# Token sums of the four-group kernel as four spread actions, fewer weight-sum steps at the end of the first FFN

## The chip, the cores and the metric

The kernel runs on one core of a Trainium2 chip. The metric is device microseconds (us) of one execution, from its start to its end on that core; lower is better. TensorE (PE) does the matrix products, VectorE (DVE) and ScalarE (ACT) the elementwise work, GpSimd (POOL) some of it and part of the DMA issuing, and SyncE (SP) issues most loads. The trace gives TensorE's granted clock as a share of full speed.

## The reference

One layer of a decoder for 512 tokens with 1024 channels, in float32:

```python
h = x + 0.5 * swiglu(rmsnorm(h, norm_ffn1), ffn1_gate, ffn1_up, ffn1_down)   # hidden width 2816
u = rmsnorm(h, norm_mix)
parts = split(u @ w_in)             # queries, keys, values, branch gates, merge gates ga and gb
o_a = compressed + selected + windowed attention (8 heads)
o_b = sliding-window attention with sinks (8 heads)
h = h + (sigmoid(ga) * (o_a @ w_branch_a) + sigmoid(gb) * (o_b @ w_branch_b)) @ w_out
h = h + 0.5 * swiglu(rmsnorm(h, norm_ffn2), ffn2_gate, ffn2_up, ffn2_down)
out = rmsnorm(h, norm_final)
# swiglu(x, wg, wu, wd) = (silu(x @ wg) * (x @ wu)) @ wd
```

## The kernel before

**Products in parts.** TensorE rounds its operands, so each float32 operand is split in two: a high part (a cast, on ACT: `whi`, `uh`, `fhi`) and a low part (the operand minus its high part, a subtraction on DVE: `wlo`, `ul`, `flo`). Each product is three matmuls (high by high, low by high, high by low). A row tile is 128 channels by 512 tokens, and `KD` = 8 row tiles make the 1024 channels; a product of one row tile over all channels (`mm3`, L387) is so 24 matmuls. The residual `h` and the scaled activations `uh`, `ul` are held as eight such tiles, channels on partitions. Results stand in banks of PSUM named `acc`, `o`, `s` and (for transposes) `tp`, two of each.

**Weights.** Every product takes a block of 128 by 1024 weights from a ring in program order: SP loads it (`raw`, L143, 0.5 MB), ACT casts it (`whi`, L151), DVE subtracts (`wlo`, L155). There are four raw buffers, so a load is issued once the block four places earlier has been split.

**The stages, in order of time.** The first FFN (FFN1) in three thirds of hidden tiles, each with a down product of eight row tiles; the projection by `w_in` and the attention, whose order of tasks on PE is a list written out by hand; the merge of the two branches; the output projection by `w_out`, row tile by row tile (`d` from 0 to 7); the second FFN (FFN2) in three thirds of hidden tiles, `TILES = (4, 5, 0, 6, 7), (8, 12, 16), (17, 21)`; and the last down product with the final norm. Every engine has its own queue and does its instructions in the order in which the program issues them; nothing is reordered.

**Norms.** As each row tile of h is ready, `norm_in(d)` issues an ACT scale (`uh`, L653), a DVE subtraction (`ul`, L654), an ACT square (L664, in a buffer named `z`, `turn_a` and so on) and a POOL addition of the square to `sqacc` (L665). After the eighth, `norm_col` sums `sqacc` over the partitions with four small matmuls into `tp`, POOL takes the power (`ny`, L678), DVE finishes, and `norm_rows` makes the row factors `r_b` by which each product is multiplied afterwards (DVE, L1808 and L1815).

**Four-groups.** In FFN2 the tiles 0, 8, 12 and 17 stand for groups of four hidden tiles. The gate and up products of such a group are done as seven half-size products in place of eight (function `four`, products at L1875), from sums of weights and from sums of tokens. Their results are turned back to the layout of the rest by 12 groups of four transposes, `turn_back()` (L1911), which later products issue in between; a dictionary such as `up_at = {2: turn_back}` says after which of the eight steps of a product something is issued.

**Weight sums.** The sums of weights are made in DRAM by the DMA queue of POOL: 48 steps of 1 MB, each a copy (L401) or a copy that accumulates (L399), from the generator `sum_steps()`. Each `next(steps)` issues one step; a step that needs an earlier one waits for it on POOL's queue. The calls stand in FFN1 (after hidden tiles over 18, four, and in the last down product at d = 1, 3, 5), in attention (24, one every so many tasks), in the output projection (d = 1, 3, 5) and in FFN2 (after each tile and inside the four-groups), which has the other 14.

**Token sums.** For each of four pairs of row tiles (k and 4 + k), `sums_of_tokens` scales both (two on ACT), makes four half-width sums (DVE, L1729, L1730, L1734, L1735) and splits them (`fhi`, L390 on ACT, and `flo`, L391 on DVE). It does this in two calls per pair: scale, two sums, split; then two sums, split. The calls for k = 0 stand behind row tile 4 of the output projection (both), those for k = 1 behind row tiles 5 and 6; those for k = 2 and 3 behind the up product of the first and the second tile of FFN2, ahead of the reading of that product's bank (`t`, L1815).

**Elsewhere.** At the end of FFN1 each row tile of h is stored to DRAM (`hd`) for the output projection, since attention takes its space: the clearing of a buffer `turn_b` (POOL, L1020) is the first to use it. In FFN2, `residual(d)` transposes a row tile of h by PE (L2008) and copies it on ACT into `o_t`, the tile of the output.

Of the kernel before, what the change touches and what calls it, by code (L numbers as in the profile page):

```python
# [362 lines left out]
def layer(ctx, tc, a, out):  # L363
# [57 lines left out]
    def sum_steps():  # L421

        for pair in ((four_steps(FOURS[0]), down_sums(0)), (four_steps(FOURS[1]), four_steps(FOURS[2])),
                     (down_sums(8), four_steps(FOURS[3]))):
            for both_steps in zip(*pair):
                for y in both_steps:
                    issue(*y)
                    yield
# [379 lines left out]
    def ffn(after, begun, side, sums, early):  # L808
# [14 lines left out]
        for third, (f0, f1) in enumerate(THIRDS):  # L823
# [30 lines left out]
            for d in range(KD):  # L854
                po = acc(False)
                mm3(po, W.next(), g_in, f1 - f0)
                if third == 2 and d < KD - 1:
                    W.prep(W.pos + W.AHEAD)
                vector.scalar_tensor_tensor(h[:, d], po, 0.5, h[:, d], op0=OP.mult, op1=OP.add)
                if third == 0:  # L860
                    if d < 3:
                        sums_of_u(0, d + 1)
                    next(side, None)
                if third == 1 and d in (0, 2, 4, 6, 7):
                    next(early, None)
                if third == 2:
                    after(d)
                    if d in (1, 3, 5):
                        next(steps, None)
# [131 lines left out]
    with ExitStack() as mixing:  # L1001
# [717 lines left out]
        def sums_of_tokens(f, p0, names):  # L1719


            k, second = f // 2, f % 2
            tt, stt = vector.tensor_tensor, vector.scalar_tensor_tensor
            if not second:
                x, y = tokens["a"] = [p0.tile([128, S], F32, name=names[0]) for _ in range(2)]
                for o, d in ((x, k), (y, 4 + k)):
                    scalar.activation(o, h[:, d], AF.Identity, scale=gains[:, 2, d:d + 1])
                p = tokens["p"] = p0.tile([128, 2, 256], F32, name=names[1])
                tt(p[:, 0], y[:, 256:], x[:, 256:], op=OP.subtract)  # L1729
                tt(p[:, 1], x[:, :256], x[:, 256:], op=OP.subtract)  # L1730
            else:
                (x, y), s1 = tokens["a"], tokens["p"][:, 0]
                p = p0.tile([128, 2, 256], F32, name=names[1])
                stt(p[:, 0], s1, -1.0, x[:, :256], op0=OP.mult, op1=OP.subtract)  # L1734
                stt(p[:, 1], y[:, :256], -1.0, p[:, 0], op0=OP.mult, op1=OP.subtract)  # L1735
            split(four_hi[:, k, 2 * second:2 * second + 2], four_lo[:, k, 2 * second:2 * second + 2], p)

        with pool("merge", 2, side="right") as mp:
# [30 lines left out]
            m_in = (lambda k: mh[:, k]), (lambda k: ml[:, k])  # L1769
            for d in range(KD):  # L1770
# [4 lines left out]
                for i in {4: (0, 1), 5: (2,), 6: (3,)}.get(d, ()):  # L1775
                    sums_of_tokens(i, mp, ("z0", "z1"))
                if d in (1, 3, 5):
                    next(steps, None)


    with pool("temp3", 2) as temp, pool("end") as end:
# [62 lines left out]
        def four(j, pairs):  # L1844
# [3 lines left out]
            slot = {5: 0, 7: 1, 6: 2, 3: 3}  # L1848
# [239 lines left out]
        for third, tiles in enumerate(TILES):  # L2088
            if third == 2:
                make_room_again()  # L2090
            for n, f in enumerate(tiles):
# [6 lines left out]
                if n > 1 or third:  # L2098
                    gate_at = {2: turn_back, 6: turn_back}
                    up_at = {2: turn_back, 6: lambda: back(3 - third)}  # L2100
                z = []
                if third < 2:
# [9 lines left out]
                mm3(pu, W.next(), u_in, KD, rows if first else up_at)  # L2112
# [3 lines left out]
                if third == 0 and n < 2:  # L2116
                    for i in (4 + 2 * n, 5 + 2 * n):
                        sums_of_tokens(i, temp, ("y", "t"))
# [6 lines left out]
                gated(z[0], pu, f - THIRDS[min(third, 2) if f != 16 else 2][0], third == 0)  # L2125
                next(steps, None)
            if third < 2:
                down()
        for _ in last:
            pass  # L2130

# [24 lines left out]
```

## Time and profile before

| | |
|---|---|
| three runs | 1148.95, 1150.98, 1152.01 us (median 1150.98) |
| the profiled execution | 1150.53 us, its span 1148.8 us, mean granted clock 0.983 |
| PE busy | 1100.0 us (96%), 5827 matmuls |
| PE loading weights (beside products) | 940.4 us (82%) |
| DVE busy | 757.2 us (66%), 1358 instructions |
| ACT busy | 541.2 us (47%), 988 instructions |
| POOL busy | 219.7 us (19%), 253 instructions |
| HBM | 260 GB/s over the span |
| the hardware queue of SP's loads | 159.98 MB, 44.1% of the 16 DMA engines' time |
| the software queue of POOL | 67.11 MB, 25.0% of the 16 DMA engines' time |
| the chain that ended last | PE 81%, DVE 7%, DMA 6%, ACT 3%, issue 2% |

PE is busy nearly throughout. A busy PE is not PE at full speed, though: where the granted clock is 0.5, a matmul takes twice as long and still counts as busy. So the waits of PE, and the clock behind each of them, are to be read together. Times in what follows count from the start of the span.

### The profile page before, as it was taken

Reading aid. Unit: us, or ns where it says so; the run is one execution under the profiler, and the core shown is the slowest. Engines: PE = TensorE matmul, PEld = TensorE weight load, DVE = VectorE, ACT = ScalarE, POOL = GpSimd, SP = SyncE. Lnnn points to the kernel's source line nnn. Section 1 sums busy time; section 2 is a strip of 40 time slices with the busy share of each in tenths; the row PEclk is TensorE's granted clock in tenths of the full one; section 3 lists DMA queues with packets and bytes.
Section 4 is the critical chain, followed back from the end, with each engine's and each line's share of the span. In section 5 each row is a group of like instructions: output and inputs, shape, how many; then the busy total and the mean of one; then the engine's idle time right before and its main releaser. Section 6 shows DMA issues by size and latency. Waiting matters only on the chain.

```text
span 1148.8 us, 15814 instructions
## 1 busy us (share of the span) xinstructions
PE 1100.0 (96%) x5827; PEld 940.4 (82%) x5827; DVE 757.2 (66%) x1358; ACT 541.2 (47%) x988; POOL 219.7 (19%) x253
## 2 busy tenths in 40 slices
PE   9999998999999799999999999979779999999987
PEld 8888898988888798998888888867557888888876
DVE  5656785854656378896777466663547876887663
ACT  5434342542434256766667543454335445464432
POOL 0312111000003035654434432112000000000002
PEclk9999999999999899999999999998899999999999
DMA  6988989798659646737899556649993555646621
GB/s 208 264 223 207 257 185 323 216 324 272 197 198 235 159 107 187 148 147 205 286 228 311 154 177 208 154 147 234 289 285 127 190 193 163 194 142 196 205 73 74
DMA packets 201414, 232.44 MB, mean 202 GB/s; under 512 B 7924, under 2 KB 152120, under 8 KB 201016
## 3 DMA queue, kind: packets, MB, share of 16 engines
q1 hardware_dynamic: 172696, 159.98, 44.1%
q0 software_dynamic: 26176, 67.11, 25.0%
q10 hardware_dynamic: 2464, 4.33, 1.0%
q8 instruction: 46, 0.75, 0.3%
q14 instruction: 32, 0.26, 0.1%
HBM read 211.47 MB, written 87.03 MB: 260 GB/s over the span
## 4 chain that ended last, share of the span: by engine, by line
PE 81%; DVE 7%; DMA 6%; ACT 3%; issue 2%; POOL 0%; POOLq 0%; ACTq 0%; DVEq 0%; SPq 0%
PE acc L387 26%; PE o L387 18%; PE s L387 17%; PE o L1875 3%; PE acc L1875 3%; PE s L1875 3%; PE o L783 2%; PE tp L1643 2%; DMA raw<-in_ffn_gate_dram 2%; DVE wlo L155 2%; PE s L783 2%; PE acc L783 2%; DMA raw<-s 1%; ACT whi L151 1%; DMA raw<-in_ffn_up_dram 1%
## 5 line engine op out<-in xcount | busy, mean ns | idle before, releaser
L155 DVE TENSOR_TENSOR wlo<-raw,whi 128x1024 fp32r<-128x1024 f32 (+2 forms) x225 | 259.7, 1174 | 104.4 <-ACT whi L151 104.1
L151 ACT CAST whi<-raw 128x1024 fp32r<-128x1024 f32 (+2 forms) x250 | 228.9, 938 | 143.4 <-PE acc L387 22.7
L387 PE MATMUL acc<-uh,whi 128*128 128x512 f32 x224 | 91.3, 408 | 1.4 <-ACT whi L151 1.4
L387 PE MATMUL acc<-uh,wlo 128*128 128x512 f32 x224 | 88.7, 396 | 0.5 <-DVE wlo L155 0.5
L387 PE MATMUL acc<-ul,whi 128*128 128x512 f32 x224 | 88.3, 394 | 0.0
L387 PE MATMUL acc<-whi,uh 128*128 128x256 f32 x224 | 65.8, 294 | 1.2 <-ACT whi L151 1.2
L387 PE MATMUL acc<-wlo,uh 128*128 128x256 f32 x224 | 63.6, 284 | 0.1
L387 PE MATMUL acc<-whi,ul 128*128 128x256 f32 x224 | 63.6, 284 | 0.0
L2053 POOL TENSOR_TENSOR o_t<-o_t,g_b 128x512 f32<-128x512 f32 (+1 forms) x5 | 5.9, 1184 | 285.7 <-ACT z L2047 285.7
L1658 DVE TENSOR_TENSOR pts<-tp,pts 128x512 fp32r<-128x512 f32 (+1 forms) x62 | 41.9, 687 | 21.3 <-ACT pts L1655 20.6
L1557 ACT ACTIVATE pbuf<-s,m 128x256 f32<-128x256 f32 (+3 forms) x96 | 47.6, 503 | 8.4 <-DVE m L1549 4.0
L387 PEld LDWEIGHTS acc<-uh,wlo 128*128 128x128 f32 x224 | 42.5, 190 | 10.6 <-DVE wlo L155 1.4
L387 PE MATMUL acc<-G,whi 128*128 128x512 f32 x164 | 50.5, 389 | 0.0
L387 PEld LDWEIGHTS acc<-uh,whi 128*128 128x128 f32 x224 | 42.8, 191 | 9.2 <-ACT whi L151 1.8
L387 PE MATMUL s<-G,whi 128*128 128x512 f32 x160 | 49.4, 390 | 0.0
L387 PE MATMUL o<-uh,whi 128*128 128x512 f32 x120 | 48.8, 407 | 0.0
L387 PEld LDWEIGHTS acc<-ul,whi 128*128 128x128 f32 x224 | 42.7, 191 | 7.4
L387 PE MATMUL o<-G,whi 128*128 128x512 f32 x156 | 48.3, 390 | 0.4 <-DVE G L768 0.4
L387 PE MATMUL o<-ul,whi 128*128 128x512 f32 x120 | 47.5, 396 | 0.0
L387 PE MATMUL o<-uh,wlo 128*128 128x512 f32 x120 | 47.3, 394 | 0.0
L1655 ACT CAST pts<-tp 128x512 fp32r<-128x512 f32 (+1 forms) x62 | 35.5, 586 | 23.8 <-PE tp L1643 18.0
L1580 POOL TENSOR_SCALAR pbuf<-pbuf,c,gate 128x256 f32<-128x256 f32 (+3 forms) x57 | 34.8, 617 | 58.4 <-DVE c L1567 37.1
(471 smaller groups left out, 3039.7 us busy)
## 6 DMA issues: line engine op xcount, KB each, us to landing
raw<-in_ffn_gate_dram SPq DMA_DIRECT2D x42, 512.0 KB, 5.8
raw<-in_ffn_down_dram SPq DMA_DIRECT2D x34, 512.0 KB, 4.6
w<-in_ffn_up_dram POOLq DMA_DIRECT2D x16, 1024.0 KB, 11.3
raw<-w SPq DMA_DIRECT2D x32, 512.0 KB, 4.2
raw<-in_ffn_up_dram SPq DMA_DIRECT2D x30, 512.0 KB, 6.0
t<-in_ffn_down_dram POOLq DMA_DIRECT2D x12, 1024.0 KB, 12.6
raw<-in_w_in_dram SPq DMA_DIRECT2D x20, 512.0 KB, 9.1
raw<-s SPq DMA_DIRECT2D x16, 512.0 KB, 5.0
```

The source lines that it names most:

```text
L151: self.nc.scalar.copy(self.place(i)[0][:, k0:k1], self.raw[i][:, k0:k1])
L155: engine.tensor_tensor(lo, self.raw[i][:, k0:k1], f32(hi), op=OP.subtract)
L387: tensor.matmul(out, lhsT, rhs, start=start, stop=stop)
L783: tensor.matmul(o, a_[:, n], x(k), start=new and n == step == 0, stop=n == 7 and step == 2, skip_group_check=True)
L1557: scalar.activation(u.p[:, hd], b.view[:, j], AF.Exp, bias=u.m[:, hd:hd + 1], scale=-1.0, accum_out=u.sum[:, hd:hd + 1])
L1580: e.tensor_scalar(u.p[:, hd], u.p[:, hd], u.c[:, hd:hd + 1], u.gate[:, hd:hd + 1], op0=OP.mult, op1=OP.mult)
L1643: tensor.transpose(ps[:w, hd], u.p[:, hd, kb * w:kb * w + w], ident)
L1655: scalar.copy(p.hi, flat(b.ps)[:w])
L1658: vector.tensor_tensor(p.lo, flat(b.ps)[:w], f32(p.hi), op=OP.subtract)
L1875: tensor.matmul(ps, x, y[:, k], start=new and kk == k == step == 0, stop=kk == k == 1 and step == 2, skip_group_check=True)
L2053: gpsimd.tensor_tensor(y, y, left["g_b"][:, cs], op=OP.mult)
```

## The change

**Token sums.** `sums_of_tokens(k, p, name)` now returns four actions for a pair: `scaled` (two on ACT), `sums` (all four half-width sums on DVE, written over the two scaled tiles), `high` (two casts on ACT) and `low` (two subtractions on DVE). The kinds and the number of the instructions stay. The actions of a pair are issued a row tile apart in the output projection: for k = 0 behind row tiles 4, 5 and 6, for k = 1 behind row tiles 5, 6 and 7. In FFN2 they stand inside the gate and up products of the first two tiles, at given steps, and behind the reading of the up product's bank. Because the sums are made in place they stand in other slots of the operand, hence the new `slot`.

**Weight sums.** In the last down product of FFN1 only d = 1 issues a step, in the output projection d = 0 too. The 48 steps keep their order, so from there on every step is issued two places later; FFN2 has one more, 15.

**The last tile.** In the last third of FFN2, the gate product of tile 21 has no turn-backs inside it; two follow behind it, as before, and the other two stand inside the up product.

```diff
--- before.py
+++ after.py
@@ -425,7 +425,7 @@
             for both_steps in zip(*pair):
                 for y in both_steps:
                     issue(*y)
-                    yield
+                    yield True
 
     steps = sum_steps()
 
@@ -865,7 +865,7 @@
                     next(early, None)
                 if third == 2:
                     after(d)
-                    if d in (1, 3, 5):
+                    if d == 1:
                         next(steps, None)
         for g in (adds, side, early):
             for _ in g:
@@ -1716,24 +1716,34 @@
 
         tokens = {}
 
-        def sums_of_tokens(f, p0, names):
-
-
-            k, second = f // 2, f % 2
+        def sums_of_tokens(k, p, name):
+
+
+            pair = []
             tt, stt = vector.tensor_tensor, vector.scalar_tensor_tensor
-            if not second:
-                x, y = tokens["a"] = [p0.tile([128, S], F32, name=names[0]) for _ in range(2)]
-                for o, d in ((x, k), (y, 4 + k)):
+
+            def scaled():
+                pair.extend(p.tile([128, S], F32, name=name) for _ in range(2))
+                for o, d in zip(pair, (k, 4 + k)):
                     scalar.activation(o, h[:, d], AF.Identity, scale=gains[:, 2, d:d + 1])
-                p = tokens["p"] = p0.tile([128, 2, 256], F32, name=names[1])
-                tt(p[:, 0], y[:, 256:], x[:, 256:], op=OP.subtract)
-                tt(p[:, 1], x[:, :256], x[:, 256:], op=OP.subtract)
-            else:
-                (x, y), s1 = tokens["a"], tokens["p"][:, 0]
-                p = p0.tile([128, 2, 256], F32, name=names[1])
-                stt(p[:, 0], s1, -1.0, x[:, :256], op0=OP.mult, op1=OP.subtract)
-                stt(p[:, 1], y[:, :256], -1.0, p[:, 0], op0=OP.mult, op1=OP.subtract)
-            split(four_hi[:, k, 2 * second:2 * second + 2], four_lo[:, k, 2 * second:2 * second + 2], p)
+
+            def sums():
+                (x1, x2), (y1, y2) = ((t[:, :256], t[:, 256:]) for t in pair)
+                tt(y2, y2, x2, op=OP.subtract)
+                tt(x2, x1, x2, op=OP.subtract)
+                stt(x1, y2, -1.0, x1, op0=OP.mult, op1=OP.subtract)
+                stt(y1, y1, -1.0, x1, op0=OP.mult, op1=OP.subtract)
+
+            def high():
+                for i, t in enumerate(pair):
+                    scalar.copy(flat(four_hi[:, k, 2 * i:2 * i + 2]), t)
+
+            def low():
+                for i, t in enumerate(pair):
+                    hi, lo = (flat(o[:, k, 2 * i:2 * i + 2]) for o in (four_hi, four_lo))
+                    tt(lo, t, f32(hi), op=OP.subtract)
+
+            return scaled, sums, high, low
 
         with pool("merge", 2, side="right") as mp:
             mh, ml = (mp.tile([128, KD, S], F32R, name=n, bufs=1) for n in ("mh", "ml"))
@@ -1767,14 +1777,18 @@
                 split(mh[:, d], ml[:, d], y)
 
             m_in = (lambda k: mh[:, k]), (lambda k: ml[:, k])
+            first_sums = []
             for d in range(KD):
                 ps = acc(False)
                 mm3(ps, W.next(), m_in, KD)
                 vector.tensor_tensor(h[:, d], ps, h[:, d], op=OP.add)
                 norm_in(d, 2)
-                for i in {4: (0, 1), 5: (2,), 6: (3,)}.get(d, ()):
-                    sums_of_tokens(i, mp, ("z0", "z1"))
-                if d in (1, 3, 5):
+                if d == 4:
+                    first_sums.extend(sums_of_tokens(k, mp, "z%d" % k) for k in range(2))
+                    a0, a1 = first_sums
+                for action in {4: (a0[0],), 5: (a0[1], a1[0]), 6: (a0[2], a1[1], a0[3]), 7: (a1[2], a1[3])}[d] if d > 3 else ():
+                    action()
+                if d in (0, 1, 3, 5):
                     next(steps, None)
 
 
@@ -1845,7 +1859,7 @@
 
 
             home = {1: "acc", 2: "acc", 5: "s", 3: "s", 6: "o", 7: "o", 4: "o"}
-            slot = {5: 0, 7: 1, 6: 2, 3: 3}
+            slot = {5: 3, 7: 1, 6: 0, 3: 2}
             p, u, w, z, back_rows = [], [], [], [], []
             made = {1: (p, "z"), 5: (w, "t"), 6: (u, "s"), 2: (z, "y")}
             col, minus = norm["col"], norm["minus"]
@@ -2095,11 +2109,17 @@
                     continue
                 first = third == n == 0
                 gate_at, up_at = {}, {}
-                if n > 1 or third:
+                if third < 2 and n > 1:
                     gate_at = {2: turn_back, 6: turn_back}
+                if third or n > 1:
                     up_at = {2: turn_back, 6: lambda: back(3 - third)}
+                if third == 0 and n < 2:
+                    now = sums_of_tokens(2 + n, temp, "y")
+                    up_at = {1: now[0], 6: rows} if first else {1: now[1], 6: now[2]}
+                    if not first:
+                        gate_at = {1: before[2], 3: before[3], 5: now[0]}
                 z = []
-                if third < 2:
+                if third < 2 and not first:
                     up_at[4] = lambda: z.append(scaled(pg))
                 pg = acc(False)
                 wp = W.next()
@@ -2109,13 +2129,10 @@
                     back(2)
                     next(last)
                 pu = acc(False)
-                mm3(pu, W.next(), u_in, KD, rows if first else up_at)
+                mm3(pu, W.next(), u_in, KD, up_at)
                 if third == 0 and n < 2:
                     for d in range(4 * n, 4 * n + 4):
                         residual(d)
-                if third == 0 and n < 2:
-                    for i in (4 + 2 * n, 5 + 2 * n):
-                        sums_of_tokens(i, temp, ("y", "t"))
                 if third == 0 and n == 1:
                     make_room()
                 if third < 2 and n + 1 == len(tiles):
@@ -2123,11 +2140,15 @@
                 if not z:
                     z.append(scaled(pg))
                 gated(z[0], pu, f - THIRDS[min(third, 2) if f != 16 else 2][0], third == 0)
+                if third == 0 and n < 2:
+                    now[1 if first else 3]()
+                    before = now
                 next(steps, None)
             if third < 2:
                 down()
         for _ in last:
             pass
+        assert next(steps, None) is None
 
 
 _INS = ["x", "positions", "norm_ffn1", "ffn1_gate", "ffn1_up", "ffn1_down", "norm_mix", "w_in", "cmp_pe_k",
```

The next rows are POOL's, at the end of FFN1, the change against before: L399 are accumulating steps of the weight sums, `w_..` and `t_..` their sums in DRAM, and L665 adds a row tile's square to the norm's sum.

```order
 L399 DMA w_5_87<-in_ffn_up_dram 512x512
-L665 TENSOR_TENSOR sqacc<-sqacc,z 128x512 x2
-L399 DMA t_0_79<-in_ffn_down_dram 512x1x512
-L665 TENSOR_TENSOR sqacc<-sqacc,z 128x512 x2
-L399 DMA w_7_88<-in_ffn_up_dram 512x512
-L665 TENSOR_TENSOR sqacc<-sqacc,z 128x512 x2
+L665 TENSOR_TENSOR sqacc<-sqacc,z 128x512 x6
 L1020 MEMSET turn_b 64x512
```

Two steps have left the queue between the additions; they are now the first that attention issues.

The next rows are DVE's in the output projection, from the sums behind row tile 5 to the addition of row tile 7, first before: `z_..` are token sums, `wlo` a weight split, `h<-o,h` and `h<-s,h` the additions of row tiles 6 and 7.

```order
L1729 TENSOR_TENSOR z_7261<-z_7258,z_7257 128x256
L1730 TENSOR_TENSOR z_7261<-z_7257 128x256
L391 TENSOR_TENSOR flo<-z_7261,fhi 128x512
L155 TENSOR_TENSOR wlo<-raw,whi 128x1024
L1773 TENSOR_TENSOR h<-o,h 128x512
L654 SCALAR_TENSOR_TENSOR ul<-h,cols_c,uh 128x512
L1734 SCALAR_TENSOR_TENSOR z_7302<-z_7261,z_7257 128x256
L1735 SCALAR_TENSOR_TENSOR z_7302<-z_7258,z_7302 128x256
L391 TENSOR_TENSOR flo<-z_7302,fhi 128x512
L155 TENSOR_TENSOR wlo<-raw,whi 128x1024
L1773 TENSOR_TENSOR h<-s,h 128x512
```

After, from the addition of row tile 6 to that of row tile 7:

```order
L1784 TENSOR_TENSOR h<-o,h 128x512
L654 SCALAR_TENSOR_TENSOR ul<-h,cols_c,uh 128x512
L1732 TENSOR_TENSOR z_7251<-z_7251,z_7250 128x256
L1733 TENSOR_TENSOR z_7250<-z_7250 128x256
L1734 SCALAR_TENSOR_TENSOR z_7250<-z_7251,z_7250 128x256
L1735 SCALAR_TENSOR_TENSOR z_7251<-z_7251,z_7250 128x256
L1744 TENSOR_TENSOR flo<-z_7207,fhi 128x512
L1744 TENSOR_TENSOR flo<-z_7208,fhi 128x512
L155 TENSOR_TENSOR wlo<-raw,whi 128x1024
L1784 TENSOR_TENSOR h<-s,h 128x512
```

Between the two additions stand four sums of one pair and two low parts of the other, where before two sums, a low part and the casts between them stood; the casts that the low parts need are issued on ACT ahead of those sums.

The last rows are DVE's in the second tile of FFN2 (tile 5), up to the first four-group, first before: `z<-s` and `t<-acc` read the banks of the gate and the up product, `t<-y` and `t<-t,y` are token sums, `g` is the gated product.

```order
L1808 TENSOR_TENSOR z<-s,r_b 128x512
L1729 TENSOR_TENSOR t<-y 128x256
L1730 TENSOR_TENSOR t<-y 128x256
L391 TENSOR_TENSOR flo<-t,fhi 128x512
L1734 SCALAR_TENSOR_TENSOR t<-t,y 128x256
L1735 SCALAR_TENSOR_TENSOR t<-y,t 128x256
L391 TENSOR_TENSOR flo<-t,fhi 128x512
L1815 TENSOR_TENSOR t<-acc,r_b 128x512
L1824 TENSOR_TENSOR g<-s,t 128x512
```

After:

```order
L1822 TENSOR_TENSOR z<-s,r_b 128x512
L1829 TENSOR_TENSOR t<-acc,r_b 128x512
L1838 TENSOR_TENSOR g<-s,t 128x512
L1848 TENSOR_TENSOR g<-g 128x256
L1850 TENSOR_TENSOR g<-g 128x256
L1851 TENSOR_TENSOR left<-g,G 128x1024
L1852 TENSOR_TENSOR g<-g 128x256
L1853 SCALAR_TENSOR_TENSOR g<-g 128x256
L1855 TENSOR_TENSOR left<-g,G 128x768
L1744 TENSOR_TENSOR flo<-y,fhi 128x512 x2
L155 TENSOR_TENSOR wlo<-raw,whi 128x1024 x4
```

The reading of the up product's bank (`t<-acc`) now follows that of the gate's directly, and the fourth pair's low parts stand behind the gating, ahead of the weight splits of the four-group.

## The prediction

> **What bounds the kernel now.** I read the page first, then who waited for whom on TensorE (PE), then the stretches around its waits, then the chain that ended last inside them.
>
> ```profile
> span 1148.8 us, 15814 instructions
> PE tp L387 <- DVE sqacc L690: 6.0, 1, 6.0
> PE tp L387 <- POOL sqacc L665: 5.8, 1, 5.8
> PE acc L1875 <- DVE t L1815: 5.5, 1, 5.5
> PE tp L1911 <- DVE t L1861: 3.7, 4, 2.8
> ```
>
> The last four lines are the longest waits of PE (us in total, times, longest). Each of the first three is a single wait, and the change edits code ahead of each. The next view gives stretches: length, then busy time of PE, PEld, DVE, ACT and POOL, then the granted clock, DMA share and GB/s.
>
> ```profile
> 355.00:382.50 27.50, 27.07 (x156) 23.78 (x155) 12.93 (x14) 9.26 (x14) 9.74 (x8) 1.00 1.11 263
> 390.60:396.60 6.00, 5.97 (x28) 5.97 (x29) 3.25 (x10) 2.91 (x6) 0.00 (x0) 0.52 0.27 81
> 774.20:784.60 10.40, 10.39 (x34) 8.61 (x35) 4.09 (x12) 0.43 (x1) 5.36 (x6) 0.62 0.70 238
> 809.10:812.80 3.70, 3.70 (x9) 2.93 (x10) 2.93 (x5) 1.04 (x1) 0.00 (x0) 0.50 1.37 495
> 1094.30:1097.10 2.80, 0.00 (x0) 0.00 (x0) 2.61 (x5) 1.33 (x2) 0.00 (x0) 1.00 0.98 313
> ```
>
> After each of the three long waits PE runs at about half clock for some us: the loss is 6.0 x 0.48 = 2.9 us, 10.4 x 0.38 = 4.0 us and 3.7 x 0.50 = 1.9 us. The 2.8 us wait near the end leaves the clock at 1.00. By the Trainium skill ("TensorE: Matmul & The Clock Gate", What's actually happening) the clock halves after an idle window of about 3.4 us and comes back after about as much work; the five rows agree.
>
> **First term: the end of the first FFN.** This is the chain into the 6.0 us wait.
>
> ```profile
> 374.24 8.32 DMA hd<-h
> ...
> 382.74 0.53 POOL turn_b L1020
> ...
> 384.76 1.05 ACT whi L151
> ...
> 388.42 1.06 POOL ny L678
> ...
> 390.29 0.30 DVE sqacc L690
> ...
> 390.63 2.07 PE tp L387 x8
> ```
>
> The last store of h took 8.32 us. Everything behind it waits: POOL clears turn_b in the space that h leaves, ACT casts zeros from it and then two weight blocks, DVE splits these, and only then comes the norm that PE needs. Why was the store slow? The stretch 355 to 382.5 has DMA at 1.11, which is full. Two of the three weight-sum steps in flight there are those that the change takes out:
>
> ```profile
> 360.20 1.22 POOL L399 DMA_DIRECT2D t<-in_ffn_down_dram  x1
> 368.76 1.03 POOL L399 DMA_DIRECT2D w<-in_ffn_up_dram  x1
> ```
>
> ```profile
> q0 software_dynamic: 1584, 3.15, 33.8%
> ```
>
> ```profile
> DMA to landing us min/median/max: 3.2/7.0/11.4
> ```
>
> The second row is the queue of the weight sums between 340 and 392 us: three steps took 33.8% of 52 us, so 5.9 us of all engines each. Without two of them 11.7 us of transfers leave the queue ahead of the store. The third row is the eight stores of h: none landed in under 3.2 us. So the store gains at most 8.32 - 3.2 = 5.1 us; I take 4.6, since the loads of w_in and the stores remain. What is late next is the same chain, 1.4 us behind PE, too short a wait to lose the clock. Gain 4.6 + 2.9 = 7.5 us; ends: 1.0 (the store waits for other traffic) and 8.0.
>
> The two steps are not gone. Every step in attention now stands two places later, so two accumulations (5.9 us of DMA each) run where copies ran, and the last of the attention's steps move to the output projection (one more there) and one into the second FFN. In attention I cost this at nothing: its PE is covered by queued work. Its price there is from -2 to +3 us.
>
> **Second term: the output projection and the first tiles of the second FFN.** The chain as it stands:
>
> ```profile
> 737.10 5.44 PE o L387 x24
> ...
> 757.80 0.72 ACT uh L653
> ...
> 760.30 0.46 DVE z L1729
> ...
> 762.74 1.23 DVE wlo L155
> 763.96 0.61 DVE h L1773
> ...
> 766.11 1.46 DVE z L1734
> ...
> 770.79 0.70 DVE h L1773
> ...
> 772.14 0.62 ACT turn_a L664
> ...
> 772.89 1.28 POOL sqacc L665
> ...
> 774.21 1.87 PE tp L387 x8
> ```
>
> ```profile
> 753.42 0.42 DVE L1734 SCALAR_TENSOR_TENSOR z<-z,z 128x256 f32<-128x256 f32 x1
> ...
> 754.99 0.69 DVE L391 TENSOR_TENSOR flo<-z,fhi 128x512 fp32r<-128x512 f32 x1 [0.69 <-ACT fhi L390]
> ```
>
> A row tile's product is 24 matmuls in 5.44 us, 0.227 us each. PE stood still from 774.2 - 5.8 = 768.4, after 18 matmuls of the next product, so the last row tile's product ended at about 764.2 and its h could have been added then; DVE did it at 770.8, since it stood behind a ping-pong of ACT and DVE that one token sum needs within one row tile (scale, subtract, cast, subtract, then the same for the second half). The number of instructions on ACT and DVE does not change; their places do. I walk DVE's new order with these durations (0.42 for a half-width sum, 0.69 for a low part, 0.72 and 0.62 for ACT's scale and square): h of tile 6 at 759.1, its ul until 761.3, four sums with about 1 us lost beside POOL's add (the 1.46 row is such a case) until 763.8, two low parts until 765.1, a weight split until 766.4, h of tile 7 until 767.0, then ACT until 768.4 and POOL until 769.7. PE waits 1.3 us and not 5.8, and the clock holds: 4.5 + 4.0 = 8.5 us.
>
> Next comes the 5.5 us wait, on DVE's reading of a product's bank, which stood behind a token sum:
>
> ```profile
> 808.44 0.61 DVE t L1815
> ...
> 816.42 9.21 DMA raw<-in_ffn_up_dram
> ```
>
> ```profile
> PE s L1875 <- DVE wlo L155: 1.0, 2, 0.5
> ```
>
> In the new order that reading comes directly behind the product, so 5.5 + 1.9 us go. But two casts of the fourth token sum now stand on ACT ahead of the copies of the transposed residual, which gives PE about 2.0 us of waiting among its transposes. And two low parts (1.4 us) stand on DVE ahead of the weight split that the group's second product needs, which with ACT's later start makes PE wait about 4.4 us there, where it waits 1.0 now (the second fence, from the waits between 800 and 830). Net 5.5 + 1.9 - 2.0 - 3.4 = 2.0. PE so reaches the second product of the first four-group 10.5 us earlier. If those 4.4 us count as one gap, the Trainium skill's rule just named halves the clock once more; an estimate from the 1.9 us row then gives 1133.5.
>
> From there on loads set the pace:
>
> ```profile
> 825.73 1.05 ACT L151 CAST whi<-raw 128x1024 fp32r<-128x1024 f32 x1 [6.79 <-DMA raw<-in_ffn_up_dram]
> 852.14 1.05 ACT L151 CAST whi<-raw 128x1024 fp32r<-128x1024 f32 x1 [2.96 <-DMA raw<-w]
> ```
>
> ```profile
> q0 software_dynamic: 4896, 14.68, 78.1%
> ```
>
> ```profile
> q0 software_dynamic: 378, 1.42, 16.0%
> ```
>
> The first two rows are the first and the last of eight weight blocks cast in that stretch: (852.14 - 825.73) / 7 = 3.8 us apart, where PE uses one in 2.72. The third row says why: between 777 and 857 us the queue of weight sums alone takes 78% of all DMA engines. POOL has nothing else to do after the norm and issues all 14 steps left as fast as they chain. The change makes that 15; the fourth row (750 to 775 us) prices a copy at 25 x 0.16 / 1.42 = 2.8 us for a MB. The flood starts with the norm, so some 4 us earlier, and ends about when it does now. What matters for PE is the spacing of its own loads, and the four-group lies inside the flood before and after. I keep 10.5 us less half of the added copy, 1.4, for its meeting the loads: 9.0 us in round figures, ends 2 and 12.
>
> **Third term: the last tile.** Four turn-backs are groups of four transposes that wait for the four-group's last gating on DVE. Two of them stood inside the gate product.
>
> ```profile
> 1097.12 0.33 PE L1911 MATMUL tp<-ident,t 128*128 128x128 f32 x1 [2.83 <-DVE t L1861]
> ```
>
> This wait began at 1094.3, six matmuls and two transposes into the gate product, which so began at about 1092.5. Now all its 24 matmuls (5.4 us) run ahead of the first transpose, until about 1098, and the gating is done by then. The other two groups move into the up product, which ends at 1098 + 5.4 + 2 for the transposes = 1105.4; their low parts stand behind three weight splits of 1.2 us on DVE and land at about 1105.8, and the last products need the first of them 9 matmuls in, at 1107.4. Gain 3.0 us (the 2.8 and a little of the other three waits), ends 1 and 3.7.
>
> **Sum.** 7.5 + 9.0 + 3.0 = 19.5 us. The profiled execution took 1150.5 us (its span and 1.7 around it), 0.5 under the median shown: 1150.5 - 19.5 + 0.5 = 1131.5 us.
>
> **Rivals.** *The flood takes the second gain back.* DMA is full from 780 to 857, so an earlier PE only waits longer for the same bytes. For it: shares above 1. Against: the loads keep 3.8 us spacing while the sums hold 78%. Gain there 2 us: 1150.5 - 7.5 - 2 - 3 + 0.5 = 1138.5. The Trainium skill ("DMA: Bandwidth & Descriptors", Queues, rings and completion order) has each engine go round the queues packet by packet; by that rule the loads keep their share however long the flood is, which speaks against this rival.
>
> *The store of h stays late*, behind w_in's loads. Gain there 1 us: 1138. For it: the stores stand among w_in's loads, and one of them took 11.4 us. Against: DMA at 1.11 with 5.9 us of it per step.
>
> *The new order keeps DVE busy past tile 7* (the four sums are a dependent chain, in place), so the 5.8 us and its clock stay: second term 0.5, 1140. For it: DVE's walk has 1.3 us of lateness already. Against: the longest ping-pong is gone from its queue.
>
> *Slower.* The flood now begins with three copies in flight and may starve PE's loads. The first four-group would have to end 23 us later than my walk has it to bring the whole to 1154.5; with eight loads that decides from (26.4 + 23) / 7 = 7.1 us between loads, near double the spacing now; at 7.5 the time is 1157. Nothing shows such a spacing.
>
> **How the numbers follow.** Forecast 0.60 (alone 1126 to 1137); flood 0.14; store 0.10; DVE 0.06; two of these together, 1143 to 1147, 0.05; better than 1122, 0.02; slower 0.03. The range 1122 to 1142 takes in the first four. 0.3% is about 3.5 us, what a measurement of this kernel tells from no change. Under 1147.5: 0.94; within: 0.03; over 1154.5: 0.03.
>
> **What would show it.** In the changed profile: the store of h landing in 3 to 5 us, and PE's wait on sqacc L690 at 1 to 2 us with no stretch near half clock behind it; PE's wait on POOL's last sqacc under 2 us; no wait of over 3 us on the reading of a bank in tile 5; new waits on the residual's copies and ahead of the group's second product; the cast of that group's eight blocks still near 3.8 us apart, ending some 9 us earlier against the last row tile; no wait of PE in the last gate product. The prediction is wrong if the store still takes 8 us, if the group's spacing grows past 5 us, or if attention loses more than 3 us to the two moved accumulations.

## The result, and the profile after

| | before | changed |
|---|---|---|
| median of six runs | 1151.49 us | 1142.13 us |
| ratio of the runs compared | 1 | 0.9918, 95% interval 0.9893 to 0.9943 |
| the profiled execution, its span | 1150.53, 1148.8 us | 1139.69, 1138.0 us |
| mean granted clock | 0.983 | 0.987 |

One run of the changed kernel took 3404.14 us; the ratio leaves it out, while the median of six takes it in (1141.34 us without it). By the ratio the change is worth 9.4 us (6.6 to 12.3), and 19.5 were forecast: 1142.13 lies just outside the range, 1122 to 1142.

Who waited for whom on PE, changed kernel (total, times, longest):

```profile
PE tp L1925 <- ACT G L1936: 9.9, 1, 9.9
PE s L1889 <- ACT whi L151: 4.7, 2, 2.9
...
PE s L1889 <- DVE wlo L155: 2.2, 2, 1.7
PE tp L387 <- POOL sqacc L665: 2.1, 1, 2.1
PE tp L2022 <- ACT o_t L2023: 1.8, 2, 1.6
```

The 6.0 us on `sqacc`, the 5.5 us on the reading of a bank and the 2.8 us in the last tile are gone, and the 5.8 us is 2.1. One wait is new and larger than any of them: 9.9 us at a turn-back (L1925). The stretches that answer to those shown of before (length, busy PE, PEld, DVE, ACT, POOL, then clock, DMA share, GB/s):

```profile
355.00:382.50 27.50, 27.07 (x160) 23.94 (x159) 15.07 (x18) 12.28 (x18) 8.27 (x8) 1.00 0.71 194
382.50:390.00 7.50, 7.50 (x66) 7.50 (x65) 5.92 (x16) 3.83 (x7) 0.00 (x0) 1.00 0.49 133
763.90:774.00 10.10, 9.86 (x55) 8.32 (x55) 6.66 (x16) 3.96 (x7) 4.36 (x5) 1.00 0.63 204
...
812.80:818.00 5.20, 4.63 (x12) 3.39 (x13) 2.78 (x3) 2.09 (x2) 1.27 (x2) 0.67 1.03 243
858.30:864.00 5.70, 5.57 (x21) 4.56 (x22) 3.50 (x7) 2.42 (x4) 0.00 (x0) 0.66 0.30 93
```

The first three had DMA at 1.11 or clocks of 0.52 and 0.62 in before. The last two are new stretches of low clock, each behind a new wait. Where the time is given back is read from the same matmul in both traces: the first product of tile 6, the tile behind the first four-group, and its third group of transposes. Before, then the changed kernel:

```profile
858.41 0.50 PE L387 MATMUL acc<-uh,whi 128*128 128x512 f32 x1 [1.35 <-ACT whi L151]
...
867.06 0.30 PE L1911 MATMUL tp<-ident,t 128*128 128x128 f32 x1 [0.90 <-ACT G L1922]
```

```profile
842.14 0.39 PE L387 MATMUL acc<-uh,whi 128*128 128x512 f32 x1
...
858.26 2.11 PE L1925 MATMUL tp<-ident,t 128*128 128x128 f32 x7 [9.93 <-ACT G L1936]
```

PE is 858.41 - 842.14 = 16.3 us ahead when it enters the tile and 867.06 - 858.26 = 8.8 us ahead within it. The chain into that wait says what held it:

```profile
836.99 18.05 DMA raw<-in_ffn_gate_dram
...
855.14 1.05 ACT whi L151
...
856.22 1.23 DVE wlo L155
857.45 1.34 DVE t L1875 x2
...
858.83 1.75 PE tp L1925 x7
```

A weight load of 0.5 MB took 18.05 us. ACT's cast of it, DVE's split and the gating that the transposes need stand behind it in their queues. The releaser that the wait names (ACT's `G`) is only the last of that chain.

The same lead along the kernel, beside what the prediction's terms add up to:

| place | lead forecast | lead measured |
|---|---|---|
| norm at the first FFN's end (390.63, 383.70) | 4.6 | 6.9 |
| attention, one matmul (455.58, 449.12) | 7.5 | 6.5 |
| norm of the second FFN (774.21, 763.90) | 12.0 | 10.3 |
| gate product of its second tile (788.85, 774.86) | 16.0 | 14.0 |
| end of the first four-group (858.41, 842.14) | 16.5 | 16.3 |
| third turn-back group of tile 6 (867.06, 858.26) | 16.5 | 8.8 |
| second four-group, one matmul (968.29, 961.06) | 16.5 | 7.2 |
| the last tile (1097.86, 1086.63) | 19.5 | 11.2 |
| end of the span (1148.8, 1138.0) | 19.5 | 10.8 |

### The profile page after: what moved, and what is told of

The parts are those of the page before. It is cut to its first block, busy times and chain, and to the rows that moved or that the text cites. A ratio compares the mean times of both kernels' runs of the same rounds, so it can differ in the third digit from the quotient of the medians.

```text
span 1138.0 us, 15818 instructions
## 1 busy us (share of the span) xinstructions
PE 1093.1 (96%) x5827; PEld 936.8 (82%) x5827; DVE 759.1 (67%) x1358; ACT 540.3 (47%) x988; POOL 219.4 (19%) x253
## 4 chain that ended last, share of the span: by engine, by line
PE 82%; DVE 7%; DMA 6%; ACT 3%; issue 2%; POOL 0%; POOLq 0%; ACTq 0%; DVEq 0%; SPq 0%
PE acc L387 27%; PE o L387 18%; PE s L387 18%; PE o L1889 4%; PE acc L1889 3%; PE s L1889 3%; PE o L783 2%; PE tp L1643 2%; DVE wlo L155 2%; DMA raw<-in_ffn_gate_dram 2%; PE s L783 2%; PE acc L783 2%; DMA raw<-s 1%; DMA raw<-in_ffn_up_dram 1%; DMA raw<-w 1%
## 6 DMA issues: line engine op xcount, KB each, us to landing
w<-in_ffn_up_dram POOLq DMA_DIRECT2D x16, 1024.0 KB, 11.7
```

## The experiments

The theory to test, "bytes": between the norm of the second FFN and the end of the weight sums DMA is full, so PE leaves that stretch when all its bytes are through, and what PE gains inside it is waited away. Its rivals: the one added step did it; the new order on ACT and DVE made the wait; the last two accumulations, which meet tile 6's loads, did it; only that place is bad.

**The parts alone.** Three kernels, each before with one part of the change.

```diff
 # steps only: end of the first FFN, output projection
-                    if d in (1, 3, 5):
+                    if d == 1:
...
-                if d in (1, 3, 5):
+                if d in (0, 1, 3, 5):
 # tokens only: sums_of_tokens and its callers as in the change
 # turn-backs only
+                    if third < 2:
+                        gate_at = {2: turn_back, 6: turn_back}
```

> The kernel before with nothing changed but the places of the weight-sum steps (two fewer at the end of the first FFN, one more in the output projection, 15 and not 14 in the second FFN). Theory 'bytes': from the norm at the start of the second FFN until the last weight sum has landed, DMA is full, so PE leaves that stretch only when the sums' bytes are through. The store of h lands 4 to 5 us sooner and PE's 6.0 us wait on sqacc L690 goes: 7.3 us. The sums then start 7.3 us earlier but have one step more, 2.8 us for a copy: they end 4.5 us earlier and the time is 1146. Rival 'the gain is kept' (the added step costs nothing): 1143. Rival 'the flood eats everything': 1150.

> The kernel before with nothing changed but the token sums in four spread actions (steps and the last tile as before). Theory 'bytes': the 5.8 us wait on POOL's sqacc shrinks to about 2.1 us, so the norm comes 3.5 us earlier and the 14 weight-sum steps with it; they end 3.5 us earlier and so does PE, whatever it gains inside: 1147. PE is some 10 us earlier at the first four-group and loses 5 to 7 us again to loads before the second down product. Rival 'my prediction's walk' (the gain is kept): 1150.5 - 10.5 = 1140. Rival 'the added step alone took the gain': also 1140, as here there are 14 steps.

> The kernel before with nothing changed but the turn-backs of the last tile (none in its gate product). All theories: the 2.8 us wait on L1911 in that product goes, 3.5 us as between the two traces: 1147. If the 3.5 us of the changed kernel came from elsewhere (weights that arrive earlier, say), no change: 1150.5.

Measured: steps 1149.24 us, ratio 0.9973 (0.9958 to 0.9988); tokens 1149.05 us, 0.9983 (0.9965 to 1.0); turn-backs 1148.36 us, 0.9959 (0.9945 to 0.9973), beside 1152.87 of before. The parts sum to 0.85% and the whole is 0.82%. The turn-backs are worth what the trace said, a little more. The other two are worth 3.1 and 2.0 us by these ratios, somewhat less than the theory expected (4.5 and 3.5), and the interval of the tokens reaches no gain at all. Each gets ahead first and gives some 10 us back in one wait, at the same turn-back, where before waited 0.9 us:

```profile
863.77 2.33 PE L1911 MATMUL tp<-ident,t 128*128 128x128 f32 x8 [10.73 <-ACT G L1922]
```

```profile
862.27 2.12 PE L1925 MATMUL tp<-ident,t 128*128 128x128 f32 x7 [11.48 <-ACT G L1936]
```

These are that turn-back with the steps alone, then with the tokens alone: the same wait, 10.7 and 11.5 us. The first keeps the old order on ACT and DVE, the second has no added step; so neither the order nor the step is needed for it.

**Pacing the sums.** The changed kernel, with the weight-sum steps of the second FFN spread.

```diff
+        def hold(x):
+            token = temp.tile([128, 4], F32, name="token")
+            vector.tensor_scalar(token, x, -1.0, None, op0=OP.mult)
+            held = temp.tile([128, 4], F32, name="held", bufs=1)
+            gpsimd.tensor_tensor(held, token, token, op=OP.add)
+            next(steps, None)
...
-                next(steps, None)
+                if first:
+                    for _ in range(3):
+                        next(steps, None)
+                else:
+                    hold(z[0][:, 0:4])
 # and hold(...) on w[1] or o_t in place of next(steps) in four() and down()
```

> The changed kernel, in which POOL issues three weight-sum steps behind the norm and then one at a time, each behind a small addition that reads what a tile of the second FFN has just made (so about one step per 12 us up to the third four-group); 15 steps in all, as before. Theory 'bytes': no stretch of full DMA is left around the first four-group, the loads land in 4 to 7 us and not 12 to 18, and the 9.9 us wait in the tile behind the group goes with its stretch of low clock, the group's own waits too: 1142 - 12 = 1130, or 1125 if nothing of it meets the later loads. Rival 'the new order of ACT and DVE makes the wait' (casts and low parts ahead of the turn-backs): the wait of 9.9 us stays, 1140 to 1142. Rival 'the sums meet the later loads': the wait goes and others of 5 us and more come between 880 and 1010 us, 1136 or more.

Measured: 1122.85 us, ratio 0.9741 (0.9721 to 0.9761). In that kernel tile 6's third turn-back group starts at 841.86 with no wait ahead of it. It beats the changed kernel by some 19 us, more than expected. The profiled executions are 16.8 us apart (spans of 1138.0 and 1121.2), and 858.26 - 841.86 = 16.4 us of that are there by this turn-back, where the theory has them. The two DMA queues (packets, MB, share of 16 engines; q0 the sums, q1 the loads) from the norm to that turn-back, before, changed and paced:

```profile
DMA packets 12676, 24.03 MB, mean 267 GB/s; under 512 B 512, under 2 KB 4608, under 8 KB 12609
...
q0 software_dynamic: 4896, 14.68, 69.4%
q1 hardware_dynamic: 7777, 9.31, 32.0%
```

```profile
DMA packets 13003, 25.18 MB, mean 277 GB/s; under 512 B 526, under 2 KB 4622, under 8 KB 12936
...
q0 software_dynamic: 5168, 15.73, 73.2%
q1 hardware_dynamic: 7832, 9.41, 31.9%
```

```profile
DMA packets 10174, 15.63 MB, mean 208 GB/s; under 512 B 383, under 2 KB 4479, under 8 KB 10171
...
q1 hardware_dynamic: 7771, 9.29, 37.5%
q0 software_dynamic: 2400, 6.29, 35.0%
```

PE needs the same 9.3 to 9.4 MB of weights to get there in all three. With 14.7 to 15.7 MB of sums beside them the shares sum to 101% and 105% for some 90 us; with 6.3 MB PE is there in 75.

**The change where no burst follows.** The same pacing on the kernel before.

```diff
 # hold() and its calls as above, in the kernel before
```

> The kernel before, with the weight-sum steps of the second FFN paced as in the paced run (three behind the norm, then one at a time); nothing else changed. It tells what the change is worth where no burst of sums follows the norm. Theory 'bytes': the burst hid the token sums' gain, so against the paced changed kernel (1122.9) all three terms of the prediction come back: 7.3 + 9 + 3.5 = 20 us, 1142 to 1143. Rival 'pacing and the change are independent': pacing takes the same 19 us off here, 1133.5, and the change is worth 10 in both.

Measured: 1141.05 us, ratio 0.9905 (0.9887 to 0.9924). So pacing alone takes 11.6 us off the kernel before, and the change is worth 1141.05 - 1122.85 = 18.2 us where the sums are paced (18.9 by the two ratios, since the kernels were not measured side by side), against 9.4 where they are not. The rival, 10 in both, falls. PE waits there for the same things as in before:

```profile
PE tp L387 <- DVE sqacc L690: 6.1, 1, 6.1
PE tp L387 <- POOL sqacc L665: 5.8, 1, 5.8
PE acc L1875 <- DVE t L1815: 5.5, 1, 5.5
PE tp L1911 <- DVE t L1861: 3.7, 4, 2.8
```

**The dose.** The changed kernel with 13 and with 17 steps left for the second FFN. In the second, the last two steps come after their sums have been read, so they don't enter the output.

```diff
-                if d in (0, 1, 3, 5):
+                if d < 6:          # 13 left
+                if d in (1, 3):    # 17 left
```

> The changed kernel with 13 and not 15 weight-sum steps left for the second FFN: two more are issued in the output projection (row tiles 0 to 5, one each). Theory 'bytes': the stretch from the first sum behind the norm to PE's leaving of the wait in the tile behind the group was 89.5 us with 14 steps and 91.5 us with 15, so about 2 us a step: 87.5 us, 1138, if the output projection bears its two more. Rival 'the last two accumulations collide with the tile's loads, however many steps come ahead': the 9.9 us wait and the 91.5 us stay, 1140 to 1142.

> The changed kernel with 17 weight-sum steps left for the second FFN: the output projection issues two (row tiles 1 and 3) and not four. Theory 'bytes': 95.5 us from the first sum to PE's leaving of the wait, 1146. Rival 'the last two accumulations, however many come ahead': 91.5 us, 1140 to 1142.

Measured: 1135.74 us, ratio 0.9855 (0.9825 to 0.9884), and 1138.3 us, 0.9876 (0.9845 to 0.9906). The first came near its 1138. The second missed 1146, since the burst did not hold 17 steps but 15:

```profile
1024.00 1.19 POOL L399 DMA_DIRECT2D t<-in_ffn_down_dram  x1 [182.92 <-DMA raw<-t]
```

The 16th waited 183 us on POOL until its sum had been read, and the last came later still. So this run has the dose of the changed kernel, without the last two accumulations in the burst, and PE still waits 4.6 us inside the four-group and 6.1 us ahead of tile 6: the last two accumulations are not needed for PE's loss. The interval of this run overlaps that of the changed kernel, so its time tells nothing more. The profiled executions together, one for each kernel, from the first sum behind the norm to tile 6's third turn-back group:

| kernel | steps, MB of sums | from, to (us) | length |
|---|---|---|---|
| 13 steps | 13, 13.63 | 768.25, 855.68 | 87.4 |
| before | 14, 14.68 | 777.37, 867.06 | 89.7 |
| tokens only | 14, 14.68 | 773.01, 862.27 | 89.3 |
| changed | 15, 15.73 | 767.30, 858.26 | 91.0 |
| steps only | 15, 15.73 | 771.89, 863.77 | 91.9 |
| 17 left, 15 in the burst | 15, 15.73 | 763.84, 853.10 | 89.3 |
| changed, paced | 6, 6.29 | 766.41, 841.86 | 75.5 |
| before, paced | 6, 6.29 | 778.87, 856.80 | 77.9 |

With a burst the length is 87 to 92 us whatever PE has gained before it; with 6 steps it is 75 to 78. More steps go with a longer stretch, 1 to 2 us each, but only roughly: the three kernels with 15 steps are 2.6 us apart, as much as a step or two, and the 1.05 MB of a step would take 3.9 us at 267 GB/s. So "bytes" names what holds PE there, and is no exact rule for the length; whether the 16 engines or the memory behind them is what is full, these runs do not separate.

**The burst at another place.** Paced, but the last 12 steps held until tile 6 and then let go at once.

```diff
-            next(steps, None)
+            for _ in range(12):
+                next(steps, None)
 # in hold(), which is called in tile 6 only
```

> The paced changed kernel, but the 12 steps that are left behind the first three are held until the tile behind the first group (tile 6) has its gate product, and then issued as fast as they chain: the same bytes in one burst, about 100 us later. Theory 'bytes' (a burst takes most of DMA wherever it stands, and the loads beside it come slower than PE needs them): PE waits in the tiles and the down product between 865 and 950 us, 10 us more than paced: 1133. Rival 'only the place behind the norm was bad, where the first four-group's weights and the first tiles' come together': 1123 as paced.

Measured: 1135.52 us, ratio 0.986 (0.9825 to 0.9894). Three stretches of it:

```profile
865.00:885.00 20.00, 20.00 (x90) 16.56 (x89) 15.21 (x21) 7.92 (x9) 2.06 (x3) 1.00 1.10 269
885.00:905.00 20.00, 13.11 (x57) 10.15 (x55) 11.20 (x13) 6.70 (x7) 2.26 (x2) 0.92 1.05 332
...
925.00:945.00 20.00, 17.62 (x71) 12.45 (x69) 10.02 (x12) 5.84 (x6) 1.02 (x1) 1.00 1.04 265
```

DMA is above 1 again and PE loses 6.9 and 2.4 us, where the paced kernel has 20.00 of 20.00 in each of these. The chain through these stretches goes back to weight loads of 11.7 to 13.2 us. A burst cost PE time at both of the places tried.

**What is left of the token sums' price.** The paced kernel, with the last pair's low parts and one weight split moved ahead in the second tile, run twice, the second time beside the paced kernel.

```diff
-                    now[1 if first else 3]()
 # now[3] and W.prep(W.pos + 2) inside gated(), behind the reading of the up product's bank
```

> The paced changed kernel, and in the second tile of the second FFN the last pair's low parts and one weight split more stand directly behind the reading of the up product's bank (before the gating), in a hole of DVE of 2.4 us. It tests the remaining price of the token sums there: the two waits of 1.7 us ahead of the first group's second product and the low clock behind them (some 2 us) go: 1122.9 - 5 = 1118. Rival 'something else is late next' (the residual's copies on ACT, the group's own loads): 1121 to 1123.

> The paced changed kernel again, on the same chip and in the same rounds as the next kernel, to tell the two apart: 1123.

> The kernel with the last low parts and one weight split moved ahead in the second tile again: by its profile 2.5 us less than the paced one, 1120.5; if the two differ only by chance, 1123.

Measured: 1120.76 us the first time; side by side 1122.94 us, ratio 0.9737 (0.9723 to 0.9752), and 1121.17 us for the paced kernel, 0.9727 (0.9713 to 0.9742). No difference can be told, and the 1118 expected was missed. Counted from the norm, PE is through the group's second product 4.7 us earlier in the first profile than in the first one of the paced kernel, and 6.2 us earlier in the second than in the second. In the first it then does not wait at tile 6's turn-back; in the second it does:

```profile
PE tp L1927 <- ACT G L1938: 3.0, 1, 3.0
```

The chain into this wait goes back to a weight load of 11.66 us, issued at 826.12, just behind a step of the sums (826.09): six steps still stand in that stretch. Why the lead of the first profile does not show in the time was not followed up. The plain paced kernel is as good as any of these versions, 1121 to 1123 us.

## Why the prediction was wrong

**First term (7.5 us): right in its mechanism, near in its sum by luck.** The last store of h, issued at 372.8, has landed by 375.55, when POOL clears the space: 2.8 us at most, for 8.32, and less than the 3.2 that the prediction took as the least a store needs. DMA is at 0.71 there for 1.11, and neither the wait nor the half clock is left, so the norm comes 6.9 us earlier (4.6 forecast) and 2.9 us of half clock go. These 9.8 are beyond the term's end of 8.0. Attention, costed at nothing, takes 3.3 of them, and the 6.5 left are near 7.5 only because the two misses cancel:

```profile
415.00:425.00 10.00, 8.06 (x56) 7.85 (x55) 6.69 (x20) 4.97 (x16) 3.47 (x3) 0.84 1.03 287
...
445.00:455.00 10.00, 9.72 (x71) 9.45 (x72) 6.85 (x26) 4.92 (x16) 2.88 (x3) 0.83 0.79 167
```

Before ran the like stretches, 425 to 435 and 445 to 455, at 1.00; the lower clock costs 1.6 and 1.7 us, the whole of it. Much of that is chance of the single profile. Five runs of the experiments (the paced kernel twice, the one with the last low parts moved ahead twice, the late burst) have the same code up to the second FFN. From the norm's first matmul at the first FFN's end to one transpose in attention (383.54 to 448.44 in the changed kernel) they took 62.5 to 64.0 us, the changed kernel 64.9, and before, less its 2.9 us of half clock, 61.6. So attention takes 0.9 to 2.4 us in those five. What pushes the clock down there was not tried.

**Second term (9.0 us): the step that failed.** Its pieces held up to the end of the four-group. POOL's last `sqacc` holds PE 2.1 us (1.3 forecast) with the clock at 1.00, the bank's wait is gone, the new waits are 1.6 us among the transposes (2.0 forecast) and 1.75 + 1.65 ahead of the second product (4.4 forecast). The group's eight blocks are cast from 811.74 to 836.82, 3.6 us apart. The lead at the group's end, 16.3 us, is that of the walk (16.5), though inside the group PE has the new wait of 2.9 us and the low clock behind it (0.67), both shown above.

The step that failed is "From there on loads set the pace", where the text kept the 10.5 us less half of a copy. It took the spacing of eight blocks as a property of the group and looked no further than its end. The casts of the three blocks behind the group, before and then changed:

```profile
857.32 1.04 ACT L151 CAST whi<-raw 128x1024 fp32r<-128x1024 f32 x1 [2.97 <-DMA raw<-in_ffn_gate_dram]
858.84 1.04 ACT L151 CAST whi<-raw 128x1024 fp32r<-128x1024 f32 x1 [0.47 <-DMA raw<-in_ffn_up_dram]
863.96 1.03 ACT L151 CAST whi<-raw 128x1024 fp32r<-128x1024 f32 x1
```

```profile
840.92 1.05 ACT L151 CAST whi<-raw 128x1024 fp32r<-128x1024 f32 x1 [1.88 <-DMA raw<-in_ffn_gate_dram]
847.82 1.05 ACT L151 CAST whi<-raw 128x1024 fp32r<-128x1024 f32 x1 [5.85 <-DMA raw<-in_ffn_up_dram]
855.14 1.04 ACT L151 CAST whi<-raw 128x1024 fp32r<-128x1024 f32 x1 [3.05 <-DMA raw<-in_ffn_gate_dram]
```

In the changed kernel they come 7 us apart, and the lead shrinks from block to block: 16.4, 11.0 and 8.8 us. By the second four-group 9.1 us are gone, of 16.3 - 6.5 = 9.8 gained since attention. The prediction itself has the flood end "about when it does now", and so it did: POOL issues the last step at 841.17 in before and at 841.19 in the changed kernel. It did not ask where PE, 16 us ahead, would then be: in tile 6, with the sums still running.

The quantity to carry through the stretch was the bytes: PE passes tile 6 only when some 24 to 25 MB are through, at 267 and 277 GB/s here, and the change moved the start of the burst (10.1 us earlier, 6.5 of these from the first term) and added a step. With 1 to 2 us for a step, as the other runs have it, the term is 10.1 - 6.5 less that, 1.6 to 2.6 us; this is worked out afterwards, from the runs. Measured, it is 8.8 - 6.5 = 2.3 at the turn-back, and 0.7 behind the low clock that follows (7.2 at the second four-group).

So the rival "the flood takes the second gain back", given 0.14 and 1138.5, is what happened; the profiled execution of the changed kernel took 1139.69. Against it stood that the loads keep their spacing. By the Trainium skill ("DMA: Bandwidth & Descriptors", Queues, rings and completion order) each engine goes round its queues by packets, which was read as: the loads keep their share however long the burst is. They do get one. Between 836 and 858 in the changed kernel it was the first row, and the second is what the paced kernel's loads took between 820 and 842, with PE waiting for none:

```profile
q1 hardware_dynamic: 3502, 2.59, 39.1%
```

```profile
q1 hardware_dynamic: 5208, 4.34, 60.5%
```

That share is two thirds of what the loads take where PE waits for none. The rule does not contradict the trace; the conclusion drawn from it did.

**Third term (3.0 us): right, a little small.** No wait of PE is left in the last gate product; the lead grows from 7.2 to 11.2, and the part alone measured 0.41% (4.7 us, interval 3.1 to 6.3). The leads so add up: 6.5 + 0.7 + 4.0 = 11.2 in the last tile, and 10.8 at the end.

**Attention's price and the rivals.** Attention's range (-2 to +3) just missed 3.3, and a loss above 3 was one of the prediction's own signs of being wrong; in the five other runs with the same code there the loss lies inside the range. "The store stays late" and "the new order keeps DVE busy" did not happen, nor did the slower case: the blocks behind the group were 7 us apart, at its threshold of 7.1, but three of them and not eight. The chances have a slip: those listed for times under 1147.5 sum to 0.97, where the text gives 0.94.

## What to carry to other kernels

Where DMA's share is 1 or more for tens of us, do not add up waits of the engine inside that stretch: count the bytes that must pass before the engine can leave it, and ask of a change whether it moves the start, the bytes or the rate. The length comes out of that only within some us. A queue that has nothing else to do issues all that it has left at once; transfers that are needed much later are to be tied to the work's progress, which here cost one small instruction on DVE and one on POOL a step and was worth twice the change itself (11.6 us on the kernel before, 19 on the changed one). And a rival that keeps the cover (here, loads) deserves its chance from the shares and not from the spacing in one place.

## What was not expected of the hardware

The same pair of waits ahead of the group's second product cost differently. In the changed kernel 1.75 and 1.65 us leave the clock at 1.00; in the paced one 1.7 and 1.7 us are followed by a clock of 0.64. The rows, changed then paced:

```profile
795.00:805.00 10.00, 6.59 (x29) 5.11 (x29) 7.88 (x9) 5.56 (x7) 0.52 (x1) 1.00 1.22 271
```

```profile
799.00:806.00 7.00, 5.17 (x13) 3.77 (x14) 5.91 (x8) 4.15 (x7) 2.20 (x2) 0.64 0.49 116
```

A wait of 2.9 us (at 809.9 in the changed kernel) was followed by 0.67, while 2.8 us in the last tile of before left 1.00. So the length of a single wait does not decide alone. Nor is the way back always the same, and the prediction's "the five rows agree" is too strong: by their lengths and mean clocks, its three rows of low clock hold about 5.8, 7.9 and 3.7 us at half. The Trainium skill ("TensorE: Matmul & The Clock Gate", What's actually happening) has the idle window run freely and not start with the wait, which fits such pairs; the 2.9 us wait, shorter than the 3.4 us that the prediction cites, it does not explain by itself, and no run here shows the window.
